# One core's decoder layer, three edits: moving operands at one offset in SBUF, state space transfers begun by Pool, exponent differences on the vector engine

## The chip, the core and the metric

The kernel runs on one core of a Trainium2 chip. The metric is the device time of one execution in microseconds (us); the profile shown here is of one execution of the kernel before the change. Lower is better.

## What is computed

The program is a chain of two transformer-like blocks on 512 tokens of width 1024, all in 32-bit floats:

```python
h = x + 0.5 * swiglu(rmsnorm(x), g1, u1, d1)                 # ffn1, hidden width 2816
# attention: compressed, selected and windowed branches (o_a), sliding window with sinks (o_b)
merged = sigmoid(ga) * (o_a @ w_branch_a) + sigmoid(gb) * (o_b @ w_branch_b)
h = h + merged @ w_out
h = h + 0.5 * swiglu(rmsnorm(h), g2, u2, d2)                 # ffn2
h = rmsnorm(h)
# second block: a gated linear recurrence of 4 heads (hgrn2) beside a state space layer (s5)
mixed = concat([hgrn2(q, f, i, g), s5(u)]) @ w_out_2
h = h + gt1 * mixed
# peer: per token and head the best 16 of 128 x 128 experts
act = gelu(einsum(h2, u_tab[idx]));  h = h + gt2 * einsum(gates * act, v_tab[idx])
out = rmsnorm(h)
```

## The kernel before

**Products.** Activations lie transposed, 8 tiles of 128 x 512 (features in partitions, tokens along them). A product with full precision is made of three passes of a faster type: an operand is split into a high part (`hi`, a cast on ACT) and a low part (`lo`, a subtraction on DVE), and `mm3` multiplies high by high, low by high and high by low. The weight tile is the stationary operand (loaded, PEld), the activation the moving one, 512 columns at a time. `weight` (L165) loads one 128 x 1024 weight tile over the SP queue, casts it on ACT (L171) and subtracts on DVE (L172). `Weights` keeps two tiles ready ahead; tiles `raw`, `whi`, `wlo` have three buffers each.

**Order.** Each stage has a main generator that issues the products and side generators that are woven in: `yield 6000` in a side generator means "go on when 6000 ns of matmul time, by the kernel's own count, have been issued". The framework under it then orders each engine's queue by its own estimates of when instructions are ready. Each engine works its queue in order, so an instruction that waits holds what stands behind it.

**Stages** (names used below, with their time in the trace): ffn1 (to 394 us), att (394 to 840), ffn2 (840 to 1247), mix (1247 to 1553), peer1 (1553 to 2440) and peer2 (to the end). Each opens a pool of SBUF tiles with `open` and closes it; the pools of all stages begin above the same resident tiles. The moving operands are:

- `xhi`, `xlo`: the normalised input of a stage, resident, used by the first products of every stage. The program lays them at byte 75,648 of each partition and on, every one 1,920 bytes past a multiple of 2,048.
- `ahi`, `alo` (ffn1, ffn2), `t` (att, mix), `pwh`, `pwl` (peer2): made inside a stage, in its pool. By the addresses that the program gives them they lie 736 (ffn1), 544 (att), 1,280 (ffn2), 928 (mix) and 704 (peer2) bytes past a multiple of 2,048.

All are 2,048 bytes a partition. Weight tiles `whi` and `wlo` lie 1,920 past a multiple of 2,048 too, and the eight 128-column slices of each follow at steps of 512 bytes.

**The end of att.** Eight branch products go into `merged`, one tile each: DVE (L812) scales, Pool (L814) adds, ACT and DVE split (L588, L589). The eight output products `wout` each need all eight `merged` tiles and begin with the first.

**The state space preparation** (`s5_prepare`) runs beside ffn2. It makes matrices for four quarters of the state space and writes them to DRAM; `s5_load` reads them back in mix. A quarter issues 24 transfers: 2 of transposed matrices (`first`), 2 of `ca`, 2 x 8 that place a triangle `ks` into a zeroed tile `T`, 2 of `T`, 1 of `cs` and 1 of `d`. All stand on ACT's queue (`nc.scalar.dma_start`; L1156 is the line of the 16). The arithmetic is Pool's (`g`) and DVE's (`v`); PE multiplies `ca` by `bz`, a spread copy of `bb`.

**The recurrence** (`hg_head`, in mix) makes for each of 4 heads and each of 7 levels two differences of a running sum (helper line L996), their exponent on ACT (L1281), and two multiplications on DVE (L1282, L1283), before PE multiplies. `s5_quarter` (four, one after another) alternates PE, DVE and Pool.

Of the kernel before, what the change touches and what calls it, by code (L numbers as in the profile page):

```python
# [8 lines left out]
F32 = mybir.dt.float32  # L9
F32R = mybir.dt.float32r  # L10
# [8 lines left out]
T = 512  # L19
D = 1024  # L20
DT = 8
# [28 lines left out]
class Prog:  # L50
# [92 lines left out]
        self.n += 1  # L143
        return f"{s}{self.n}"

    def open(self, name):
        self.phase_cm = self.tc.tile_pool(name=name, bufs=1, reuse_waits="tile")
        self.ph = self.phase_cm.__enter__()

    def close(self):  # L150
        self.phase_cm.__exit__(None, None, None)
# [542 lines left out]
    def attention(self, st, done):  # L694
        nc, A, ph = self.nc, self.A, self.ph
# [48 lines left out]

        sg, merged = [[], []], []

        def main():
            win = A["win_t"]
            order = [win[i] for i in range(8)] + [(A["win_n"][c], 688) for c in range(4)]
# [4 lines left out]
            W = Weights(self, order)  # L754
# [50 lines left out]
            for b, key, o in ((1, "ob", ob), (0, "oa", oa)):  # L805
                yield has(key)
                for m in range(DT):
                    ps = self.ps()
                    w = next(W)
                    yield from self.product(ps, w, o)  # L810
                    x = sg[b][m]
                    nc.vector.scalar_tensor_tensor(x, x, 1.0, ps, op0=ALU.add, op1=ALU.mult)  # L812
                    if b == 0:
                        nc.gpsimd.tensor_tensor(x, x, sg[1][m], op=ALU.add)  # L814
                        hl = self.t2k(F32R), self.t2k(F32R)
                        self.split(x, *hl)
                        merged.append(hl)
            for m in range(DT):
                ps = self.ps()
                w = next(W)  # L820
                yield from self.product(ps, w, merged)
                done(m, ps)
# [193 lines left out]
    def s5_prepare(self):  # L1016
# [81 lines left out]
        yield 8000  # L1098
        for i in range(2):
            s = slice(64 * i, 64 * i + 64)  # L1100
            v.tensor_copy(bz[s, :, :, 16 * i:16 * i + 16], bb[s])
        di = ph.tile([32, 16, 16], F32, name="di")
        v.tensor_tensor(di, m["eye16"][:, None, :].to_broadcast([32, 16, 16]),
                        m["s5d"][:, :, None].to_broadcast([32, 16, 16]), op=ALU.mult)
        for j in range(4):
            q = slice(4 * j, 4 * j + 4)
            first, second = self.s5d[j]
            sh = [128, 4, 8, 16]
            f4 = lambda t: t.rearrange("p (g l h) -> p g l h", g=4, l=8)
            pr, pi = (pd[:, i, :, q].rearrange("p l g -> p g l")[:, :, :, None].to_broadcast(sh) for i in range(2))  # L1110
            br, bi = (bb[:, i, q, :][:, :, None, :].to_broadcast(sh) for i in range(2))
            t, R = self.t2k(), [self.t2k(), self.t2k()]
            self.mul(g, f4(R[0]), pr, br)
            self.mul(g, f4(t), pi, bi)
            self.sub(g, R[0], R[0], t)
            self.mul(g, f4(R[1]), pr, bi)
            self.mul(g, f4(t), pi, br)
            self.add(g, R[1], R[1], t)
            yield 20000
            for i in range(2):  # L1120
                ps = self.ps()
                for a in range(4):
                    s = slice(a * 128, (a + 1) * 128)
                    self.tr(ps[:, s], R[i][:, s], self.ident)
                o = self.t2k()
                self.evac(o, ps)
                nc.scalar.dma_start(first[:, 512 * i:512 * i + 512], o)
            sh = [128, 4, 9, 16]
            pr, pi = (pw[:, i, :, q].rearrange("p l g -> p g l")[:, :, :, None].to_broadcast(sh) for i in range(2))
            pnb = pn[:, :, q].rearrange("p l g -> p g l")[:, :, :, None].to_broadcast(sh)  # L1130
            cr, ci = (m["s5c"][:, i, q, :][:, :, None, :].to_broadcast(sh) for i in range(2))
            ca = [ph.tile(sh, F32, tag="ca", bufs=3, name=self.name("ca")) for _ in range(3)]
            flat = lambda t: t.rearrange("p g l h -> p (g l h)")
            self.mul(g, ca[0], pr, cr)
            self.mul(g, ca[2], pi, ci)
            self.sub(g, flat(ca[0]), flat(ca[0]), flat(ca[2]))
            self.mul(g, ca[1], pnb, cr)
            self.mul(g, ca[2], pr, ci)
            self.sub(g, flat(ca[1]), flat(ca[1]), flat(ca[2]))
            yield 22000  # L1140
            for i in range(2):
                nc.scalar.dma_start(second[:, 1024 + 576 * i:1600 + 576 * i], flat(ca[i]))
            ps = self.ps()
            for a in range(4):
                o = ps[0:32, a * 128:(a + 1) * 128]
                for i in range(2):
                    self.mm(o, lhsT=bz[:, i, 4 * j + a, :], rhs=ca[i][:, a, 0:8, :], start=(i == 0), stop=(i == 1))
            ks = self.t2k()[0:32].rearrange("p (g x) -> p g x", g=4)
            v.tensor_copy(ks, ps[0:32].rearrange("p (g x) -> p g x", g=4))
            v.tensor_tensor(ks[:, :, 0:16], ks[:, :, 0:16], di[:, q, :], op=ALU.add)  # L1150
            for i in range(2):
                T = self.t2k()
                g.memset(T, 0.0)
                tv = T.rearrange("p (g x) -> p g x", g=4)
                for l in range(8):
                    nc.scalar.dma_start(tv[16 * l:16 * l + 16, :, 16 * l:128], ks[16 * i:16 * i + 16, :, 0:128 - 16 * l])  # L1156
                nc.scalar.dma_start(second[:, 512 * i:512 * i + 512], T)
            yield 6000

            a, k = self.t2k(), self.t2k()  # L1160
            f3 = lambda t: t.rearrange("p (g c) -> p g c", c=64)
            ang = a[:, 0:256]
            v.tensor_tensor(f3(ang), m["r8"][:, q, None].to_broadcast([128, 4, 64]),
                            m["iota"][:, None, :].to_broadcast([128, 4, 64]), op=ALU.mult)
            cs = self.t2k()
            for i, turn in enumerate((0.25, 0.0)):
                yield 4000
                self.reduce_angle(a[:, 256:512], ang, k[:, 0:256], turn)
                nc.scalar.activation(cs[:, i * 256:(i + 1) * 256], a[:, 256:512], AF.Sin)
            nc.scalar.dma_start(first[:, 1024:1536], cs)  # L1170
            d = self.t2k()
            dv = d.rearrange("p (i g c) -> p i g c", i=2, g=4)
            v.tensor_copy(dv, m["rho"][:, None, q, None].to_broadcast([128, 2, 4, 64]))
            v.memset(dv[:, :, :, 0:1], 0.0)
            nc.scalar.dma_start(first[:, 1536:2048], d)
            yield 6000


# [9 lines left out]
    def s5_quarter(self, j, un, r, ys):  # L1188
# [8 lines left out]
                                 rhs=self.ident[:, lp:128:2], start=True, stop=True)  # L1197
        U = self.t2k()
        self.evac(U, ps)
        yield 1000  # L1200
        ps = self.ps()
        for i in range(2):
            for gq in range(8):
# [1 line left out]
                self.mm(ps[64 * g2:64 * g2 + 64, i * 256 + a * 64:i * 256 + a * 64 + 64],  # L1205
                                 lhsT=r["RT"][i][:, a * 128 + 64 * g2:a * 128 + 64 * g2 + 64],
                                 rhs=U[:, gq * 64:gq * 64 + 64], start=True, stop=True)
        yield 0
        cos = r["cs"][:, None, 0:256].to_broadcast([128, 2, 256])
        sin = r["cs"][:, None, 256:512].to_broadcast([128, 2, 256])  # L1210
        h2 = lambda t: t.rearrange("p (i x) -> p i x", i=2)
        a, b, z, x = self.t2k(), self.t2k(), self.t2k(), self.t2k()
        v.tensor_tensor(h2(a), h2(ps), cos, op=ALU.mult)
        v.tensor_tensor(h2(b), h2(ps), sin, op=ALU.mult)
        self.add(g, z[:, 0:256], a[:, 0:256], b[:, 256:512])
        self.sub(g, z[:, 256:512], a[:, 256:512], b[:, 0:256])
        v.tensor_tensor_scan(x, r["d"], z, 0.0, op0=ALU.mult, op1=ALU.add)
        a, b, z = self.t2k(), self.t2k(), self.t2k()
        v.tensor_tensor(h2(a), h2(x), cos, op=ALU.mult)
        self.mul(g, h2(b), h2(x), sin)  # L1220
        zv, av, bv = i4(z), i4(a), i4(b)
        g.memset(zv[:, :, :, 0:1], 0.0)
        self.sub(g, zv[:, 0, :, 1:64], av[:, 0, :, 0:63], bv[:, 1, :, 0:63])
        self.add(g, zv[:, 1, :, 1:64], av[:, 1, :, 0:63], bv[:, 0, :, 0:63])
        yield 8000
        yn = ph.tile([64, 8, 8, 16], F32, tag="yn", bufs=1, name=self.name("yn"))
        for g2 in range(2):
            ps = self.ps()
# [36 lines left out]
    def hg_head(self, hd, q, k, b, vn, os, have_v):  # L1265
# [6 lines left out]
        def level(l):  # L1272
# [3 lines left out]
            mid = bv[:, :, 0, H - 1:H].to_broadcast([128, 256 // H, H])  # L1276
            e = self.t2k()
            ev = blk(e)
            self.sub(g, ev[:, :, 0, :], mid, bv[:, :, 0, :])
            self.sub(g, ev[:, :, 1, :], bv[:, :, 1, :], mid)  # L1280
            nc.scalar.activation(e, e, AF.Exp)  # L1281
            v.tensor_tensor(ev[:, :, 0, :], blk(k)[:, :, 0, :], ev[:, :, 0, :], op=ALU.mult)  # L1282
            v.tensor_tensor(ev[:, :, 1, :], blk(q)[:, :, 1, :], ev[:, :, 1, :], op=ALU.mult)  # L1283
# [9 lines left out]
        for l in range(7):  # L1293
# [7 lines left out]
            if l == 3:  # L1301
# [4 lines left out]
                v.tensor_copy(dec, qe[:, 127:512:128])  # L1306
                v.tensor_tensor(qe, qe, q, op=ALU.mult)
                last = c4(b)[:, :, 127:128].to_broadcast([128, 4, 128])
                self.sub(g, c4(kd), last, c4(b))
                nc.scalar.activation(kd, kd, AF.Exp)  # L1310
                v.tensor_tensor(kd, kd, k, op=ALU.mult)
            yield 2200
# [289 lines left out]
    def peer(self, st, done):  # L1602
# [2 lines left out]
        self.gd = self.dram.tile([T // GB, 128, 128, GB], F32, name="gates_d")  # L1605
        NE = 128
        gs = [self.dram.tile([128, 512], F32, name=f"act_d{e}") for e in range(NE)]
        self.open("peer1")
        self.n_t2k = 6
        xs = []  # L1610
        box = {}
# [29 lines left out]
        self.spawn(work())  # L1641
        self.weave(early())
        self.close()
        self.open("peer2")
        self.n_t2k = 4
        f = lambda x: x.rearrange("p (b t) -> p b t", t=GB)
        gts, acts = {}, {}
# [59 lines left out]
def program(tc, A, out, dbg=None, stop=None):  # L1707
    with ExitStack() as ctx:
# [3 lines left out]
        h = [P.const.tile([128, 512], F32, name=f"h{d}") for d in range(DT)]  # L1712
        rope_cm = tc.tile_pool(name="rope", bufs=1, reuse_waits="tile")
        P.rp = rope_cm.__enter__()
        P.open("ffn1")
        st = P.norm_start()
        W = P.ffn_weights(A["g1"], A["u1"], A["d1"])
        for d in range(DT):
# [12 lines left out]
            P.dump(f"h1_{d}", h[d])  # L1731
        if stop == "ffn1":
            return
        P.open("att")
        P.n_t2k = 44
        P.active = 2
        P.att_order = [3, 2, 4, 5, 6, 7, 1, 0]
# [12 lines left out]
            P.dump(f"h2_{d}", h[d])  # L1750
        if stop == "att":
            return
        P.open("ffn2")
        P.n_t2k = 9
        P.mid_start(vec["norm_final"], vec["norm_mix_w_2"])
        W = P.ffn_weights(A["g2"], A["u2"], A["d2"])
# [5 lines left out]
        P.weave(P.ffn(h, st3, W,  # L1762
                      lambda m, half: P.mid_tile(m, half, h, vec["norm_final"], vec["norm_mix_w_2"], st4), halves=True))
        P.close()
        P.open("mix")
        P.n_t2k = 31
        P.mix_consts()
        st5 = {"hi": [], "lo": [], "ready": []}
# [142 lines left out]
```

## Time and profile before

| | us |
|---|---|
| median of 3 runs | 3177.6 (3174.46 to 3178.54) |
| the profiled execution, its own time | 3182.49 |
| span from its first to its last instruction | 3180.5 |

| engine | busy us | share of the span |
|---|---|---|
| PE (matmul) | 3061.3 | 96% |
| DVE | 2044.6 | 64% |
| ACT | 1164.7 | 37% |
| POOL | 1084.8 | 34% |

The granted TensorE clock has a mean of 0.98 of full speed over the span. Matmuls overlap in the profile (a 512-column one lasts some 390 ns and the next starts after some 230), so their pace is read from start to start.

### The profile page before, as it was taken

Reading aid. Unit: us, or ns where it says so; the run is one execution under the profiler, and the core shown is the slowest. Engines: PE = TensorE matmul, PEld = TensorE weight load, DVE = VectorE, ACT = ScalarE, POOL = GpSimd, SP = SyncE. Lnnn points to the kernel's source line nnn. Section 1 sums busy time; section 2 is a strip of 40 time slices with the busy share of each in tenths; the row PEclk is TensorE's granted clock in tenths of the full one; section 3 lists DMA queues with packets and bytes.
Section 4 is the critical chain, followed back from the end, with each engine's and each line's share of the span. In section 5 each row is a group of like instructions: output and inputs, shape, how many; then the busy total and the mean of one; then the engine's idle time right before and its main releaser. Section 6 shows DMA issues by size and latency. Waiting matters only on the chain.

```text
span 3180.5 us, 39943 instructions
## 1 busy us (share of the span) xinstructions
PE 3061.3 (96%) x14672; PEld 2493.6 (78%) x14672; DVE 2044.6 (64%) x3733; ACT 1164.7 (37%) x1851; POOL 1084.8 (34%) x993
## 2 busy tenths in 40 slices
PE   8999998889999999999999988999999999999998
PEld 7888875567777778878888777888887788888887
DVE  7445466754657565864665899888883666555653
ACT  4222334442422224543433343445453333322332
POOL 1000110001222222431254689878771533223321
PEclk9999999999999999989999999999999999999999
DMA  6344331112435444221333344555556765555642
GB/s 197 118 131 136 94 96 47 34 47 86 160 101 170 131 141 133 85 77 54 100 121 116 103 150 168 189 188 188 191 186 225 244 200 184 185 194 193 201 135 78
DMA packets 145059, 443.53 MB, mean 139 GB/s; under 512 B 20177, under 2 KB 22257, under 8 KB 139745
## 3 DMA queue, kind: packets, MB, share of 16 engines
q1 hardware_dynamic: 82512, 285.41, 28.0%
q10 hardware_dynamic: 51968, 111.57, 9.7%
q0 software_dynamic: 10384, 44.01, 4.5%
q8 instruction: 116, 1.90, 0.2%
q14 instruction: 79, 0.64, 0.1%
HBM read 361.88 MB, written 77.86 MB: 138 GB/s over the span
## 4 chain that ended last, share of the span: by engine, by line
PE 78%; DVE 11%; issue 4%; ACT 2%; POOL 2%; DMA 2%; ACTq 0%; SPq 0%; DVEq 0%; POOLq 0%
PE ps L82 77%; DVE wlo L172 2%; DVE b L1543 1%; PE ps L86 1%; DMA aw<-ada_w 1%; ACT whi L171 1%; DVE stage L1568 1%; DMA act_d<-t 1%; DVE sel L1526 0%; DVE mx L896 0%; POOL t L814 0%; DVE aa L521 0%; ACTq L1156 0%; POOL a L1542 0%; DVE eq L1519 0%
## 5 line engine op out<-in xcount | busy, mean ns | idle before, releaser
L171 ACT CAST whi<-raw 128x1024 fp32r<-128x1024 f32 (+2 forms) x505 | 516.6, 1025 | 1210.2 <-PE ps L82 918.3
L82 PE MATMUL ps<-xhi,whi 128*128 128x512 f32 (+1 forms) x2232 | 879.0, 395 | 26.0 <-ACT whi L171 14.5
L82 PE MATMUL ps<-xhi,wlo 128*128 128x512 f32 (+1 forms) x2232 | 868.1, 390 | 8.2 <-DVE wlo L172 8.2
L82 PE MATMUL ps<-xlo,whi 128*128 128x512 f32 (+1 forms) x2232 | 869.4, 390 | 0.8 <-DVE xlo L380 0.7
L172 DVE TENSOR_TENSOR wlo<-raw,whi 128x1024 fp32r<-128x1024 f32 (+2 forms) x470 | 596.7, 1270 | 161.2 <-ACT whi L171 151.4
L82 PEld LDWEIGHTS ps<-xhi,whi 128*128 128x128 f32 x2232 | 425.4, 191 | 117.2 <-ACT whi L171 15.4
L82 PEld LDWEIGHTS ps<-xhi,wlo 128*128 128x128 f32 x2232 | 424.3, 190 | 99.3 <-DVE wlo L172 10.5
L82 PEld LDWEIGHTS ps<-xlo,whi 128*128 128x128 f32 x2232 | 425.2, 191 | 81.4 <-issue 2.1
L1542 POOL TENSOR_SCALAR a<-iota,routeT 128x128 fp32r<-128x128 f32 x512 | 439.6, 874 | 103.1 <-PE ps L82 97.2
L82 PE MATMUL ps<-pwl,whi 128*128 128x512 f32 (+1 forms) x1048 | 408.6, 390 | 2.8 <-DVE pwl L589 2.8
L82 PE MATMUL ps<-pwh,whi 128*128 128x512 f32 (+1 forms) x1048 | 406.8, 388 | 3.3 <-ACT pwh L588 3.2
L82 PE MATMUL ps<-pwh,wlo 128*128 128x512 f32 (+1 forms) x1048 | 403.1, 385 | 0.0
L1660 POOL TENSOR_TENSOR t<-t,gt 128x512 f32<-128x512 f32 x128 | 201.5, 1593 | 419.2 <-DMA t<-act_d 317.7
L1543 DVE SCALAR_TENSOR_TENSOR b<-iota,routeT,routeG 128x256 fp32r<-128x256 f32 x512 | 251.8, 541 | 46.0 <-PE ps L82 46.0
L82 PEld LDWEIGHTS ps<-pwh,whi 128*128 128x128 f32 x1048 | 197.4, 188 | 48.1 <-ACT pwh L588 4.6
L1794 DVE SCALAR_TENSOR_TENSOR h<-ps,mod,h 128x512 f32<-128x512 f32 (+1 forms) x131 | 96.3, 735 | 214.8 <-PE ps L82 214.8
L82 PEld LDWEIGHTS ps<-pwl,whi 128*128 128x128 f32 x1048 | 197.6, 189 | 42.3 <-DVE pwl L589 4.5
L82 PEld LDWEIGHTS ps<-pwh,wlo 128*128 128x128 f32 x1048 | 197.4, 188 | 42.5 <-DVE wlo L172 0.4
L1567 ACT COPY stage<-ps 128x256 f32<-128x256 f32 x256 | 138.1, 643 | 174.3 <-PE ps L82 138.1
L589 DVE TENSOR_TENSOR pwl<-t,pwh 128x512 fp32r<-128x512 f32 x128 | 144.8, 1160 | 40.0 <-ACT pwh L588 35.9
L266 POOL TENSOR_TENSOR acc<-acc,sq 128x512 f32<-128x512 f32 x18 | 32.3, 1796 | 391.2 <-ACT sq L262 390.8
L1568 DVE TENSOR_TENSOR stage<-stage,ps 128x256 f32<-128x256 f32 x256 | 147.3, 623 | 8.2 <-ACT stage L1567 8.1
(401 smaller groups left out, 3859.6 us busy)
## 6 DMA issues: line engine op xcount, KB each, us to landing
raw<-pu SPq DMA_DIRECT2D x128, 512.0 KB, 3.5
raw<-pv SPq DMA_DIRECT2D x128, 512.0 KB, 3.5
act_d<-t ACTq DMA_DIRECT2D x128, 256.0 KB, 2.4
gates_d<-stage ACTq DMA_DIRECT2D x32, 1024.0 KB, 4.6
gt<-gates_d POOLq DMA_DIRECT2D x16, 2048.0 KB, 14.6
t<-act_d ACTq DMA_DIRECT2D x128, 256.0 KB, 3.6
aw<-ada_w SPq DMA_DIRECT2D x48, 512.0 KB, 4.5
raw<-g SPq DMA_DIRECT2D x44, 512.0 KB, 3.6
```

The source lines that it names most:

```text
L82: self.nc.tensor.matmul(out, lhsT=lhsT, rhs=rhs, start=start, stop=stop)
L86: self.nc.tensor.transpose(out, x, ident)
L171: nc.scalar.copy(hi[:, :n], raw[:, :n])
L172: (nc.gpsimd if self.pool_lo else nc.vector).tensor_tensor(lo[:, :n], raw[:, :n], hi[:, :n].bitcast(F32), op=ALU.subtract)
L266: nc.gpsimd.tensor_tensor(st["acc"], st["acc"], sq, op=ALU.add)
L589: self.nc.vector.tensor_tensor(lo, x, hi.bitcast(F32), op=ALU.subtract)
L1542: g.tensor_scalar(a[:, i, :], iota, T2[0][:, c], None, op0=ALU.is_equal)
L1543: v.scalar_tensor_tensor(b[:, i], iota[:, None, :].to_broadcast([128, 2, 128]), T2[1][:, c], TG[:, t + i, :, None].to_broadcast([128, 2, 1 ...
L1567: nc.scalar.copy(sv, pv[:, :, 0])
L1568: v.tensor_tensor(sv, sv, pv[:, :, 1], op=ALU.add)
L1660: g.tensor_tensor(f(t), f(t), gts[e // 8][:, :, e % 8, :], op=ALU.mult)
L1794: nc.vector.scalar_tensor_tensor(x, ps, P.mod[:, 40 + d:41 + d], x, op0=ALU.mult, op1=ALU.add)
```

## The change

1. `open` takes a number of bytes and lays an unused tile `pad` of that size first in each stage's pool, so that all later tiles of the pool move up: ffn1 by 1,184, att by 1,376, ffn2 by 640, mix by 992, peer1 by 128, peer2 by 1,216 bytes. In ffn1, att, ffn2, mix and peer2 the moving operands of the stage then lie 1,920 bytes past a multiple of 2,048.
2. At the end of att the split of a `merged` tile becomes a side generator that goes on 3400 ns later, and the first two `wout` products are made together: first tiles 0 to 5 of both, then tiles 6 and 7 of both.
3. The 24 transfers of a quarter in `s5_prepare` go from ACT's queue to Pool's, two copies into `bz` from DVE to Pool, and waits in matmul time change (20000 to 13000, 22000 to 15000, a new 5000 ahead of each sine).
4. `s5_quarter` gets other and more places at which it yields.
5. In `hg_head` the two differences of each level and one of 128 x 512 per head go from Pool to DVE.

```diff
-    def open(self, name):
+    def open(self, name, pad):
         self.phase_cm = self.tc.tile_pool(name=name, bufs=1, reuse_waits="tile")
         self.ph = self.phase_cm.__enter__()
+        self.ph.tile([128, pad // 4], F32, name="pad")
...
+        def halves(x):
+            yield 3400
+            hl = self.t2k(F32R), self.t2k(F32R)
+            self.split(x, *hl)
+            merged.append(hl)
...
                         nc.gpsimd.tensor_tensor(x, x, sg[1][m], op=ALU.add)
-                        hl = self.t2k(F32R), self.t2k(F32R)
-                        self.split(x, *hl)
-                        merged.append(hl)
-            for m in range(DT):
+                        self.spawn(halves(x))
+
+            ws, pss = [W.take(hold=True) for _ in range(2)], [self.ps(), self.ps()]
+            for ks in (range(6), range(6, 8)):
+                for m in range(2):
+                    _, hi, lo = ws[m]
+                    for k in ks:
+                        if len(merged) <= k:
+                            yield lambda: len(merged) > k
+                        s = slice(k * 128, (k + 1) * 128)
+                        self.mm3(pss[m], hi[:, s], lo[:, s], merged[k][0], merged[k][1], k == 0, k == 7)
+                        if k % 2:
+                            yield
+                    if k == 7:
+                        W.prep()
+                        done(m, pss[m])
+            for m in range(2, DT):
...
-            v.tensor_copy(bz[s, :, :, 16 * i:16 * i + 16], bb[s])
+            g.tensor_copy(bz[s, :, :, 16 * i:16 * i + 16], bb[s])
...
-            yield 20000
+            yield 13000
...
-                nc.scalar.dma_start(first[:, 512 * i:512 * i + 512], o)
+                g.dma_start(first[:, 512 * i:512 * i + 512], o)
...
-            yield 22000
+            yield 15000
...
-                    nc.scalar.dma_start(tv[16 * l:16 * l + 16, :, 16 * l:128], ks[16 * i:16 * i + 16, :, 0:128 - 16 * l])
-                nc.scalar.dma_start(second[:, 512 * i:512 * i + 512], T)
+                    g.dma_start(tv[16 * l:16 * l + 16, :, 16 * l:128], ks[16 * i:16 * i + 16, :, 0:128 - 16 * l])
+                g.dma_start(second[:, 512 * i:512 * i + 512], T)
...
                 self.reduce_angle(a[:, 256:512], ang, k[:, 0:256], turn)
+                yield 5000
                 nc.scalar.activation(cs[:, i * 256:(i + 1) * 256], a[:, 256:512], AF.Sin)
...
-        yield 1000
+        yield 2400
...
-        yield 0
+        yield 700
...
+        yield 1700
         self.add(g, z[:, 0:256], a[:, 0:256], b[:, 256:512])
         self.sub(g, z[:, 256:512], a[:, 256:512], b[:, 0:256])
+        yield 1800
         v.tensor_tensor_scan(x, r["d"], z, 0.0, op0=ALU.mult, op1=ALU.add)
...
+        yield 1600
         self.mul(g, h2(b), h2(x), sin)
...
-        yield 8000
+        yield 4500
...
-            self.sub(g, ev[:, :, 0, :], mid, bv[:, :, 0, :])
-            self.sub(g, ev[:, :, 1, :], bv[:, :, 1, :], mid)
+            self.sub(v, ev[:, :, 0, :], mid, bv[:, :, 0, :])
+            self.sub(v, ev[:, :, 1, :], bv[:, :, 1, :], mid)
...
-                self.sub(g, c4(kd), last, c4(b))
+                self.sub(v, c4(kd), last, c4(b))
...
-        self.open("peer1")
+        self.open("peer1", 128)
...
-        self.open("peer2")
+        self.open("peer2", 1216)
...
-        P.open("ffn1")
+        P.open("ffn1", 1184)
...
-        P.open("att")
+        P.open("att", 1376)
...
-        P.open("ffn2")
+        P.open("ffn2", 640)
...
-        P.open("mix")
+        P.open("mix", 992)
```

## Rows read from the trace of the kernel before

**Rows 1.** The page's chain of work that ended last, by engine.
```profile
PE 78%; DVE 11%; issue 4%; ACT 2%; POOL 2%; DMA 2%; ACTq 0%; SPq 0%; DVEq 0%; POOLq 0%
```

**Rows 2.** Busy time by stage: length, engines' busy us (count), granted clock, DMA.
```profile
394.00:840.00 446.00, 410.08 (x1979) 295.52 (x1979) 265.57 (x603) 181.05 (x457) 42.49 (x28) 0.95 0.21 65
840.00:1247.00 407.00, 392.13 (x1826) 322.62 (x1825) 251.43 (x373) 119.72 (x159) 96.86 (x80) 0.98 0.45 140
1247.00:1553.00 306.00, 290.14 (x1858) 244.30 (x1857) 194.41 (x346) 138.62 (x212) 91.13 (x112) 0.95 0.26 86
2480.00:3180.00 700.00, 691.91 (x3103) 570.65 (x3101) 404.84 (x400) 206.25 (x256) 216.67 (x138) 1.00 0.55 179
```

**Rows 3.** Timeline of PE: starts of resident operands' matmuls (start us, us).
```profile
330.17 0.39 PE L82 MATMUL ps<-xhi,whi 128*128 128x512 f32 x1
...
335.61 0.39 PE L82 MATMUL ps<-xhi,whi 128*128 128x512 f32 x1
```

**Rows 4.** Timeline of PE: starts of the stages' own operands' matmuls (ffn1, att, peer2).
```profile
206.43 0.40 PE L82 MATMUL ps<-ahi,wlo 128*128 128x512 f32 x1
...
211.34 0.40 PE L82 MATMUL ps<-ahi,wlo 128*128 128x512 f32 x1
...
805.15 0.64 PE L82 MATMUL ps<-t,whi 128*128 128x512 f32 x2
...
811.48 0.63 PE L82 MATMUL ps<-t,whi 128*128 128x512 f32 x2
...
2600.40 0.39 PE L82 MATMUL ps<-pwh,whi 128*128 128x512 f32 x1
...
2605.90 0.39 PE L82 MATMUL ps<-pwh,whi 128*128 128x512 f32 x1
```

**Rows 5.** Waits of PE from 762 to 840 us (total us, times, longest).
```profile
PE ps L82 <- ACT t L588: 4.7, 2, 2.7
```

**Rows 6.** Busy time and granted clock behind four waits, columns as in rows 2.
```profile
795.00:802.00 7.00, 4.33 (x10) 2.78 (x10) 3.89 (x5) 2.69 (x4) 2.17 (x1) 0.52 0.25 80
886.00:898.00 12.00, 7.42 (x22) 5.60 (x21) 9.93 (x9) 3.64 (x5) 10.23 (x8) 0.72 0.19 65
...
1128.00:1140.00 12.00, 6.78 (x19) 4.61 (x18) 10.75 (x15) 4.92 (x7) 7.07 (x5) 0.72 0.42 136
...
1403.00:1423.00 20.00, 20.00 (x101) 14.06 (x102) 8.58 (x15) 6.27 (x11) 3.46 (x5) 0.50 0.17 57
```

**Rows 7.** Waits of PE, then of DVE, in ffn2.
```profile
PE ps L82 <- DVE wlo L172: 8.9, 4, 4.6
PE ps L82 <- ACT whi L171: 5.5, 3, 4.9
...
DVE bbz L1101 <- POOL bb L999: 7.5, 1, 7.5
```

**Rows 8.** The 64 triangle transfers on ACT's queue, and who waited for them.
```profile
L1156 ACTq DMA_DIRECT2D t<-t x64: 567/607/1572, 962.3 to 1207.8; - x64
...
  ACT ahi L588: 29.9, 2
```

**Rows 9.** Groups on POOL: issuing transfers (busy us, mean ns | idle before).
```profile
L1652 POOL DMA_DIRECT2D gt<-gates_d x16 | 27.6, 1726 | 52.2 <-DMA act_d<-t 45.8 <-DMA t<-act_d 2.9 <-POOL t L1660 2.4
...
L1183 POOL DMA_DIRECT2D s5y<-s5m x4 | 2.3, 564 | 16.1 <-PE ps L82 16.1
```

**Rows 10.** Waits of PE in mix.
```profile
PE ps L82 <- DVE t L1283: 5.5, 3, 3.8
```

**Rows 11.** Groups of the recurrence: differences on POOL, multiplications on DVE.
```profile
L996 POOL TENSOR_TENSOR t<-t 128x256 f32<-128x256 f32 x56 | 38.7, 720 | 36.1 <-DVE t L1256 36.1
...
L1282 DVE TENSOR_TENSOR t<-t,t 128x256 f32<-128x256 f32 x28 | 18.1, 648 | 10.3 <-ACT t L1281 10.3
```

**Rows 12.** Timeline in mix: L1282 with Pool at work, and without.
```profile
1289.95 0.86 DVE L1282 TENSOR_TENSOR t<-t,t 128x256 f32<-128x256 f32 x1
...
1305.42 0.41 DVE L1282 TENSOR_TENSOR t<-t,t 128x256 f32<-128x256 f32 x1
```

More of the change, by code (lines that the diff above doesn't have):

```diff
@@ L1139, in s5_prepare @@
             self.sub(g, flat(ca[1]), flat(ca[1]), flat(ca[2]))
-            yield 22000
+            yield 15000
             for i in range(2):
-                nc.scalar.dma_start(second[:, 1024 + 576 * i:1600 + 576 * i], flat(ca[i]))
+                g.dma_start(second[:, 1024 + 576 * i:1600 + 576 * i], flat(ca[i]))
             ps = self.ps()
@@ L1168, in s5_prepare @@
                 self.reduce_angle(a[:, 256:512], ang, k[:, 0:256], turn)
+                yield 5000
                 nc.scalar.activation(cs[:, i * 256:(i + 1) * 256], a[:, 256:512], AF.Sin)
-            nc.scalar.dma_start(first[:, 1024:1536], cs)
+            g.dma_start(first[:, 1024:1536], cs)
             d = self.t2k()
@@ L1174, in s5_prepare @@
             v.memset(dv[:, :, :, 0:1], 0.0)
-            nc.scalar.dma_start(first[:, 1536:2048], d)
+            g.dma_start(first[:, 1536:2048], d)
             yield 6000
```

## The prediction

> **What bounds the kernel now.** I read the page first. TensorE is the engine of 78% of the chain that ended last, and the other engines' shares are a few waits, not a second bound [rows 1]. So a saving must come from three places: a shorter spacing between matmuls, less waiting of PE, or less time at a low granted clock. I then read the stages as windows: att, ffn2 and mix leave PE idle for 36, 15 and 16 us and have mean clocks of 0.95, 0.98 and 0.95, while peer2 leaves 8 us at 1.00 [rows 2]. Next I took PE's timeline where it waits for nothing, since matmuls overlap and only starts show their pace; then the waits of PE in the three stages; then the clock right behind the longest of them; last the groups of ACT, Pool and DVE that the change touches.
>
> **Edit 1, the pads.** A resident operand's 24 matmuls take 5.44 us from first to last start: 226.7 ns each [rows 3]. A stage's own operands are slower: 21 in 4.91 us in ffn1 (233.8 ns), 27 in 6.33 us in att (234.4), 24 in 5.50 us in peer2 (229.2) [rows 4]. All are 512 columns wide at full clock. The one difference that I find in the program is the offset. If the pads give every operand 226.7 ns, 528 products of ffn1 (22 tiles x 8 x 3), 384 of att, 456 of ffn2 and 168 of mix, counted from the loops, gain 7.1 to 7.7 ns each (ffn2 and mix priced by ffn1 and att), 11.2 us; peer2's 3,000 gain 2.5 ns each, 7.5 us. That is 18.7 us. Where PE waits for something else the gain is lost, so I take 17.5. The lower end is 0, because offset 704 (peer2) costs 2.5 ns and offset 736 (ffn1), 32 bytes from it, costs 7.1: offset alone does not order them. For peer1's one-hot operands and the half-width products no row shows a pace against an offset; 932 matmuls by the largest difference seen, 7.7 ns, bound them at 7 us either way. I take 0.
>
> The Trainium skill, "SBUF — State Buffer", section "Who interferes with whom", says that PE and ACT never wait on anyone there. By that sentence an operand's place would not matter, and the 17.5 would be 0. The rows above show a pace that differs by operand, which the sentence does not explain; they do not show that place is the reason.
>
> **Edit 2, the end of att.** PE waits 4.7 us there for ACT's split of the merged tiles [rows 5]. The split waits for Pool's addition to the same tile, 2.17 us for one, and from 795 to 802 us the granted clock is 0.52 while PE is busy for 4.33 us [rows 6]; at full clock that work takes 2.25 us, so 2.1 more are lost. Together 6.8. After the change 2 x 6 x 3 = 36 matmuls (8.2 us at 226.7 ns) need only the first six tiles. What is late next is the last merged tile: Pool's 2.17 us, then a cast and a subtraction; if each took as long as the addition, 6.5 in all, below 8.2. The new 3400 ns gap is matmul time, and it takes the split out from ahead of later branch work in ACT's and DVE's queues. I take 6.5; the ends are 0 (the split itself becomes late) and 7.
>
> **Edit 3, Pool issues the transfers.** In ffn2 PE waits 8.9 us for `wlo` and 5.5 for `whi` [rows 7]. The longest of these have one kind of cause. ACT's queue holds 64 triangle transfers of 0.607 us, 39 us of issuing, in a row and behind landings; an `ahi` cast there waited 29.9 us in two waits [rows 8], and weight casts stand behind it. And DVE's copy into `bz` stood 7.5 us waiting for Pool [rows 7] with a weight subtraction behind it. Behind two of these the clock is 0.72 for 12 us each [rows 6]: with levels of 1.2 and 2.4 GHz, half and full speed, that is 6.7 us at half, worth 3.4 us, twice. So 14.4 + 6.8 = 21.2 us can be had. Nothing on PE's weight path remains behind a transfer.
>
> What it costs: Pool gets 96 issues. No row shows these on Pool. The nearest are 0.564 us (4 of `s5y`, the same kind of small copy between tile and DRAM) and 1.726 us (`gt`, the dearest that Pool issues) [rows 9]. I take 0.56: 54 us onto Pool's 97 busy of 407 [rows 2]; at 1.73 it is 166 and Pool still fits. But behind an issue that waits for a landing now stand `ca`, the next quarter's arithmetic and the fills of `T`, and PE's products of `ca` wait for these. `ca` is due 15000 ns of matmul time after its start, not 22000. I allow 1 us of PE's waiting in each quarter, 4 in all; if the cover is gone (Pool late by a whole 0.56 x 16 = 9 us in each quarter) it is 36. The two `bz` copies are 2 us on an idle Pool, hidden. I take 21.2 - 4, rounded up to 18 for the smaller waits of the same kind; ends -15 and 22.
>
> The same page of the Trainium skill, section "SBUF: two separate sides", warns against transfers from Pool's queue: while VectorE holds the shared port pair, descriptors can't be written, and it gives about 620 ns alone and 3100 overlapped. An estimate by that page: 96 x 2.5 us = 240 us more on Pool. The 0.564 us of `s5y`, taken in mix with DVE at work, does not show it; four issues are few.
>
> **Edits 4 and 5, mix.** The stage lasts 306 us and PE is busy for 290.1 at a mean clock of 0.95 [rows 2]. PE's largest wait is 3.8 us for `t` of L1283 [rows 10], near 1397 us: the recurrence's differences stand on Pool behind an addition of `s5_quarter` that waits for DVE, the exponents behind these, the multiplications behind those. From 1403 to 1423 the clock is 0.50 [rows 6], which loses 10 us. So 14 us hang on this one place, and all idle time with all clock loss (306 x 0.05) is 31.
>
> The price: 56 differences leave Pool, where they took 38.7 us (720 ns), with 36.1 us of waits [rows 11]. On DVE the nearest form is L1282, same shape: 0.86 us with Pool at work, 0.41 without [rows 12]. So DVE gains 56 x 0.41 = 23 to 56 x 0.65 = 36 us, and some 3 for the four 128x512 ones. In return the multiplications, 648 ns in the mean [rows 11], fall towards 410 when Pool is not beside them: 56 x 0.24 = 13 us back. Net 13 to 27 us on DVE's 194.4 of 306 [rows 2], which is room in the mean. The new wait: a multiplication behind the exponent on ACT, after two differences on the same queue. Queued behind it on DVE are weight subtractions; PE has them ready two tiles ahead. The longer yields of `s5_quarter` come to some 4 us a quarter, 15 in all, and finish before the last products need the result as long as the quarters don't end the stage. I take 10 of the 14; the ends are -10 and +27.
>
> **Sum.** 17.5 + 6.5 + 18 + 10 = 52 us. The profiled execution took 3182.5 (span 3180.5 and 2.0 around it), so it would come to 3130.5. The median of the runs shown is 4.9 below the profiled one, so 52 less than 3177.6 is 3125.6: 3126.
>
> **Rivals.**
>
> *A. The pads do nothing*: the slow pace belongs to the tiles (their writers, the mix of work beside them), not to the place. For: 704 and 736 bytes price so differently; against: the operands of ffn1 and att are slow by nearly the same, in the company of very different work. 52 - 17.5 = 34.5: 3143.
>
> *D. DVE becomes the bound in mix*: each level's chain of two differences, exponent and two multiplications is now DVE, ACT, DVE, and DVE's weight subtractions stand behind. It decides where PE's lead of two weight tiles (48 matmuls, 11 us at 226.7 ns) is less than what DVE has queued. Then DVE's 27 us come onto the path in place of the 10: 52 - 37 = 15: 3163. For: DVE is the busiest engine beside PE; against: 64% busy.
>
> *C. Pool's issue is dear, slower than before.* Pool has 407 - 97 = 310 us free in ffn2. With the 29.9 us that ACT waited behind landings [rows 8] it becomes the end of ffn2 from (310 - 30) / 96 = 2.9 us an issue. At 3.5 us: 97 + 30 + 336 = 463, 56 more than the stage, and the 18 are not won: 3126 + 18 + 56 = 3200. For: no row shows the triangle form on Pool, with starts in the middle of the partitions; against: both rows of issues on Pool lie below 1.8 us.
>
> *E. Another order on the queues*: a place in ffn2 or mix gets a new wait with 10 us of half clock behind it, as the old one had. It takes the size of one place, 14 us: 3140, inside the forecast's range.
>
> **Chances.** The forecast with E 0.62 (own range 3108 to 3146), A 0.17, D 0.14 (with A also, 3180, no change), C 0.07. Low end: all bounds in favour, 18.7 + 7 + 22 + 27 = 75, gives 3103; rounded to 3100 for the half-width products. High end: D's 3163 with 3 for a Pool a little late, 3166. A difference under 0.2%, 6.4 us, is about what a measurement here cannot tell from no change. Slower needs C's turning point (0.07, less a small part that only eats the gain): 0.06. Same: D with A, and C near its turning point: 0.05. Faster: 0.89.
>
> **What the profile after would show.** Pads: starts of `ahi`, `t`, `pwh` 226 to 227 ns apart; if still 234, A. Att: no wait of PE for L588 near 790 to 800 us and no stretch at 0.52. Ffn2: no L1156 on ACT's queue, that line on Pool near 0.56 us; PE's waits for `wlo` and `whi` below 5 us together, the 0.72 stretches gone; a wait of PE for `ca` or `ks` of over 4 us a quarter makes edit 3 wrong, as does an issue of over 2.9 us. Mix: L1282 near 410 ns, DVE's busy time at 207 to 221 us, no stretch of 20 us at 0.50; a wait of PE for DVE that is longer than 5.5 us in sum makes edit 5 wrong. The step I trust least is that offset alone sets the pace; the next is that mix gets no new wait in the place of the old.

## The result

The changed kernel takes 3136.44 us (median of 4 runs, 3134.93 to 3138.35), the kernel before 3178.07 beside it (4 runs): ratio 0.9867, interval 0.9849 to 0.9885, or 41.6 us less. The forecast was 3126 in a range of 3100 to 3166. The profiled execution took 3137.6; its span is 3135.8.

The chain of work that ended last, by engine (of the changed kernel, as in [rows 1]):

```profile
PE 84%; DVE 10%; ACT 2%; issue 2%; DMA 1%; POOL 1%; SPq 0%; ACTq 0%; DVEq 0%; POOLq 0%
```

PE's share of the chain grew from 78% to 84%. Where the time went is seen by stages. For the table I took PE's timeline and measured from landmark to landmark: first `ahi` matmul, last `ahi` matmul of ffn1, last `t` by `wlo` matmul of att, last `ahi` of ffn2, last `t` by `wlo` of mix, first `pwh` matmul, last one. Each row is the one profiled execution of a kernel (us), the last column the median of all its runs; all but `before` and `after` are experiments of the next section.

| kernel | ffn1 | att | ffn2 | mix | peer1 | peer2 | median of all runs |
|---|---|---|---|---|---|---|---|
| before | 302.6 | 454.0 | 408.9 | 297.2 | 910.3 | 713.5 | 3178 |
| pads_only | 299.2 | 446.4 | 405.8 | 288.2 | 910.7 | 707.1 | 3165.7 |
| att_only | 302.6 | 448.1 | 407.8 | 293.5 | 909.3 | 713.3 | 3173.7 |
| prep_only | 302.6 | 453.4 | 389.9 | 295.9 | 910.6 | 715.0 | 3161.8 |
| mix_only | 302.6 | 453.1 | 408.8 | 287.2 | 910.7 | 713.3 | 3171.2 |
| after | 299.2 | 448.4 | 387.2 | 286.8 | 911.5 | 707.1 | 3136.4 |
| no_pads | 302.6 | 452.7 | 390.4 | 287.0 | 910.1 | 713.0 | 3147.3 |
| heads01_pool | 299.2 | 447.2 | 387.1 | 280.0 | 911.6 | 707.5 | 3128.8 |

From before to after: ffn1 -3.4, att -5.6, ffn2 -21.7, mix -10.4, peer1 +1.2, peer2 -6.4. By the forecast's terms the savings were 3.7, 9.5, 21.2, 11.3, 0 and 7.5. The six differences come to 46.3 us, more than the 41.6 of the medians: the profiled execution of the kernel before was 4.4 us above its median, that of the changed kernel 1.1.

In the changed kernel line numbers are larger by 2 from L149 on, by more behind the later edits: L588 is L590, L1156 is L1178, L1282 and L1283 are L1308 and L1309, L996 is L1018, L1300 is L1326. Its windows of the same stages (columns as in [rows 2]; the last one is a stretch early in mix):

```profile
391.00:832.00 441.00, 409.36 (x1981) 297.26 (x1980) 266.20 (x606) 181.59 (x457) 42.14 (x27) 0.95 0.21 66
832.00:1217.00 385.00, 381.40 (x1823) 318.02 (x1822) 256.70 (x368) 119.67 (x158) 153.37 (x179) 1.00 0.47 148
1217.00:1503.00 286.00, 272.94 (x1787) 232.26 (x1786) 196.49 (x388) 136.69 (x202) 45.31 (x49) 0.97 0.26 88
2440.00:3130.00 690.00, 687.25 (x3109) 572.19 (x3107) 402.13 (x394) 206.06 (x257) 215.00 (x138) 1.00 0.56 180
1284.00:1302.00 18.00, 13.17 (x54) 11.10 (x54) 16.60 (x38) 4.44 (x13) 0.00 (x0) 0.62 0.18 62
```

Ffn2 has PE idle for 3.6 us in place of 14.9, at a clock of 1.00. Pool's busy time there went from 96.9 to 153.4 us: 52 us of the 96 issues (the forecast added 54) and 2.3 of the two copies. Mix keeps a weak place, from 1284 to 1302 us. So does the end of att. These are the same 15 us there before and after:

```profile
790.00:805.00 15.00, 10.08 (x33) 6.90 (x32) 7.87 (x10) 5.18 (x7) 4.35 (x2) 0.77 0.35 121
```

```profile
790.00:805.00 15.00, 13.33 (x51) 10.30 (x50) 8.25 (x10) 6.77 (x9) 4.35 (x3) 0.89 0.43 141
```

A mean clock of 0.77 is 6.9 us at half clock, 0.89 is 3.3: about half of that loss is left.

The pace (starts of the stages' own operands, answering to [rows 4]):

```profile
206.16 0.39 PE L82 MATMUL ps<-ahi,whi 128*128 128x512 f32 x1
...
211.60 0.39 PE L82 MATMUL ps<-ahi,whi 128*128 128x512 f32 x1
...
809.91 0.62 PE L82 MATMUL ps<-t,whi 128*128 128x512 f32 x2
...
815.35 0.62 PE L82 MATMUL ps<-t,whi 128*128 128x512 f32 x2
...
2599.74 0.39 PE L82 MATMUL ps<-pwh,whi 128*128 128x512 f32 x1
...
2605.18 0.39 PE L82 MATMUL ps<-pwh,whi 128*128 128x512 f32 x1
```

All three are 24 matmuls in 5.44 us, 226.7 ns each, the figure of the resident operands [rows 3]. The waits of PE at the end of att, in ffn2 and in mix (columns as in [rows 5]):

```profile
PE ps L82 <- ACT t L590: 1.4, 1, 1.4
PE ps L82 <- DVE wlo L174: 0.8, 1, 0.8
...
PE ps L82 <- DVE wlo L174: 3.0, 2, 2.0
PE ps L82 <- DVE alo L591: 0.6, 1, 0.6
...
PE ps L82 <- DVE t L1326: 5.3, 3, 2.6
PE ps L82 <- DVE t L1309: 3.2, 2, 2.0
```

The groups of the moved work, on Pool in ffn2 and on DVE in mix, as in [rows 9, 11]:

```profile
L1178 POOL DMA_DIRECT2D t<-t x64 | 34.3, 543 | 17.1 <-DVE t L568 17.1
...
L1018 DVE TENSOR_TENSOR t<-t 128x256 f32<-128x256 f32 x56 | 20.8, 416 | 0.0
L1308 DVE TENSOR_TENSOR t<-t,t 128x256 f32<-128x256 f32 x28 | 12.7, 453 | 0.6 <-ACT t L1307 0.4
L1309 DVE TENSOR_TENSOR t<-t,t 128x256 f32<-128x256 f32 x28 | 12.2, 435 | 0.0
...
L1018 DVE TENSOR_TENSOR t<-t 128x512 f32<-128x512 f32 x4 | 2.7, 682 | 0.0
```

An issue takes 0.543 us on Pool (forecast 0.56), a difference 0.416 on DVE (0.41), and the multiplications of both lines fell from 36.0 us in 56 (18.1 and, for L1283, 17.9; 644 ns) to 24.9 (444 ns).

### The profile page after: what moved, and what is told of

It reads as the page before. It is cut to its first block, busy times and chain, and to the rows that moved or that the text cites. A ratio compares the mean times of both kernels' runs of the same rounds, so it can differ in the third digit from the quotient of the medians.

```text
span 3135.8 us, 39961 instructions
## 1 busy us (share of the span) xinstructions
PE 3035.7 (97%) x14672; PEld 2489.8 (79%) x14672; DVE 2059.1 (66%) x3791; ACT 1168.3 (37%) x1853; POOL 1100.6 (35%) x1031
## 4 chain that ended last, share of the span: by engine, by line
PE 84%; DVE 10%; ACT 2%; issue 2%; DMA 1%; POOL 1%; SPq 0%; ACTq 0%; DVEq 0%; POOLq 0%
PE ps L82 83%; DVE wlo L174 2%; DVE b L1569 2%; PE ps L86 1%; DVE stage L1594 1%; DVE sel L1552 1%; ACT whi L173 1%; DVE mx L918 0%; DMA act_d<-t 0%; POOL t L823 0%; DVE eq L1545 0%; POOL a L1568 0%; ACT t L923 0%; ACT t L590 0%; DVE ps L914 0%
## 5 line engine op out<-in xcount | busy, mean ns | idle before, releaser
L82 PEld LDWEIGHTS ps<-xhi,whi 128*128 128x128 f32 x2232 | 424.3, 190 | 110.4 <-DVE stage L1594 10.4
L1568 POOL TENSOR_SCALAR a<-iota,routeT 128x128 fp32r<-128x128 f32 x512 | 446.0, 887 | 98.1 <-PE ps L82 92.3
L591 DVE TENSOR_TENSOR pwl<-t,pwh 128x512 fp32r<-128x512 f32 x128 | 152.8, 1223 | 43.5 <-ACT pwh L590 39.6
```

The costliest lines, as they stand in the source:

```text
L82: self.nc.tensor.matmul(out, lhsT=lhsT, rhs=rhs, start=start, stop=stop)
L591: self.nc.vector.tensor_tensor(lo, x, hi.bitcast(F32), op=ALU.subtract)
L1568: g.tensor_scalar(a[:, i, :], iota, T2[0][:, c], None, op0=ALU.is_equal)
```

## The experiments

**The pads, alone and left out.**

```diff
 # pads_only: before, with
+        self.ph.tile([128, pad // 4], F32, name="pad")
 # no_pads: after, without that line
```

> The kernel before with the pads alone. Theory (the place of a stage's operand sets its pace): all 512-column products of ahi, t, pwh and pwl start 226 to 227 ns apart; some 18 us less than before, of which 3.5 in ffn1, 6 to 7.5 in peer2, 1 to 3 in each of the others; the waits of PE for ACT and DVE in att, ffn2 and mix stay. Rival (the pads work only together with the other edits, or the order of the queues changes with them): a saving under 10 us, or one that does not lie in ffn1 and peer2.

> The changed kernel without its pads. If the parts add up, it is 18 us slower than the changed kernel, 3155 us, with the paces of before (234 and 229 ns) and without the waits that edits 2 to 5 removed. Rival (a shorter matmul only gives PE more to wait for in the stages that wait): 8 to 12 us slower, since only ffn1 and peer2 pay.

pads_only: 3165.66 us against 3177.64, ratio 0.9962 (0.9948 to 0.9976), 12.0 us less. no_pads: 3147.34, 10.9 us above the changed kernel. So the pads are worth 11 to 12 us, the figure of the rival for no_pads (8 to 12) and not 18. In the two pairs of the table ffn1 gains 3.4 and 3.4, ffn2 3.1 and 3.2, peer2 6.4 and 5.9, so ffn2 pays too. Att shows 7.6 and 4.3, but more than its pad differs there: its granted clock from 394 to 840 us is 0.97 in pads_only and 0.95 in the kernel before. Mix gains nothing from its pad when edits 4 and 5 are there (286.8 and 287.0). The 9 us that mix lost in the profile of pads_only are chance: of its five runs the profiled one took 3155.1, the others 3163.8 to 3166.1. In it the longest wait, 3.8 us, is still there, but the 20 us behind it have a clock of 0.91, not 0.50 [rows 6]. The wait (L1285 is L1283 of the kernel before), then the window behind it:

```profile
1387.38 1.96 PE L82 MATMUL ps<-t 128*128 128x128 f32 x8 [3.81 <-DVE t L1285]
```

```profile
1387.00:1407.00 20.00, 19.52 (x170) 14.94 (x171) 12.78 (x22) 8.69 (x14) 5.35 (x7) 0.91 0.23 83
```

**What the offset is measured against.** Two kernels move the weights or the operands.

```diff
 # wswap: after, with
-        self.w = ep(tc.tile_pool(name="w", bufs=3))
         self.big = ep(tc.tile_pool(name="big", bufs=1))
+        self.w = ep(tc.tile_pool(name="w", bufs=3))
-        self.open("peer2", 1216)
+        self.open("peer2", 0)
 # offs: after, with pads of
-    1184 (ffn1), 1376 (att),  640 (ffn2),  992 (mix), 1216 (peer2)
+    1696 (ffn1),  864 (att), 1664 (ffn2), 1120 (mix), 1280 (peer2)
```

> The changed kernel with the weight tiles laid behind the resident tiles, so that weights lie 704 past a multiple of 2048 and xhi, xlo, ahi, t still 1920; peer2 has no pad, so that pwh and pwl lie at 704, as the weights. If the pace goes by the moving operand's own place: 226.7 ns for xhi and ahi, 226 to 232 for pwh and pwl, as before. If it goes by the distance of operand and weights: 226.7 for pwh and pwl, 229 to 234 for xhi and ahi, and some 20 us slower than the changed kernel.

> The changed kernel with other pads, so that the operand lies behind the weight tile's place, taken modulo 2048, by 512 bytes in ffn1, 1536 in att, 1024 in ffn2, 128 in mix and 64 in peer2 (0 in the changed kernel). If only the same place modulo 2048 is fast: 229 to 237 ns in all five stages, some 18 us slower than the changed kernel. If the eight slices of a weight tile, 512 bytes apart, are what counts: 226.7 ns in ffn1, att and ffn2, 228 to 234 in mix and peer2, 6 to 9 us slower.

wswap took 3166.3 us (one run), 30 more than the changed kernel where some 20 were expected. PE's timeline of it, `xhi` in ffn1 and `pwh` in peer2:

```profile
329.94 0.39 PE L82 MATMUL ps<-xhi,whi 128*128 128x512 f32 x1
...
335.54 0.39 PE L82 MATMUL ps<-xhi,whi 128*128 128x512 f32 x1
...
2609.95 0.39 PE L82 MATMUL ps<-pwh,whi 128*128 128x512 f32 x1
...
2615.39 0.39 PE L82 MATMUL ps<-pwh,whi 128*128 128x512 f32 x1
```

`xhi` has not moved modulo 2,048 and is now slow: 24 in 5.60 us, 233.3 ns. `pwh` lies at 704, where it was slow before, and is fast: 24 in 5.44 us, 226.7 ns, because the weights lie at 704 too. So the pace goes by the distance between operand and weight tile. offs took 3146.8 us (one run), 10 more than the changed kernel where 6 to 9 were expected, and its timeline says which distances are fast (in this order: ffn1 at 512, att at 1,536, ffn2 at 1,024, mix at 128, peer2 at 64):

```profile
206.27 0.39 PE L82 MATMUL ps<-ahi,whi 128*128 128x512 f32 x1
...
211.71 0.39 PE L82 MATMUL ps<-ahi,whi 128*128 128x512 f32 x1
...
810.23 0.62 PE L82 MATMUL ps<-t,whi 128*128 128x512 f32 x2
...
815.67 0.62 PE L82 MATMUL ps<-t,whi 128*128 128x512 f32 x2
...
1173.64 0.39 PE L82 MATMUL ps<-ahi,whi 128*128 128x512 f32 x1
...
1179.08 0.39 PE L82 MATMUL ps<-ahi,whi 128*128 128x512 f32 x1
...
1475.10 0.62 PE L82 MATMUL ps<-t,whi 128*128 128x512 f32 x2
...
1479.75 0.62 PE L82 MATMUL ps<-t,whi 128*128 128x512 f32 x2
...
2609.98 0.39 PE L82 MATMUL ps<-pwh,whi 128*128 128x512 f32 x1
...
2615.48 0.39 PE L82 MATMUL ps<-pwh,whi 128*128 128x512 f32 x1
```

Distances of 512, 1,024 and 1,536 keep 226.7 ns (24 in 5.44 us); 128 gives 232.5 (20 in 4.65), 64 gives 229.2 (24 in 5.50). Multiples of 512, the step of the weight tile's slices, are the fast ones among the distances tried; none was a multiple of 256 alone, so whether that would do is not shown.

**Edit 2 alone.**

> The kernel before with edit 2 alone (split of the merged tiles as a side generator, two output products made together). The forecast's sum says 6.5 us less. By the changed kernel's profile, where one wait for the split is left with 3.4 us of half clock, 3 to 5 us less: 3173 to 3175 us. Rival (the stage's gain in the changed kernel is its pad's): no change within 2 us.

3173.66 us against 3178.33, ratio 0.9987 (0.9973 to 1.0001): 4.7 us, and an interval that just touches no change. Eight of its ten runs lie below all 19 of the kernel before. From 790 to 805 us the clock of its profiled execution is 1.00, where the kernel before has 0.77; one wait of 1.3 us for the split is left. In the changed kernel the same edit leaves a clock of 0.89 there. The time of the whole stage decides little here: att_only and no_pads run the same att, and it takes 448.1 and 452.7 us.

**Edit 3, alone and with its transfers back on ACT.**

```diff
 # prep_only: before, with edit 3; act_dma: after, with (and so for all 24)
-                    g.dma_start(tv[...], ks[...])
+                    nc.scalar.dma_start(tv[...], ks[...])
```

> The kernel before with the state space transfers on Pool and the waits in matmul time changed, nothing else. Theory (ACT's and DVE's queues held up the weights): ffn2 loses 17 to 20 us, the rest stays, 3158 to 3161 us. Rival (ffn2's gain in the changed kernel came from the pads and the new order): under 10 us.

> The changed kernel with the 24 transfers of a quarter back on ACT's queue; the new waits in matmul time and Pool's two copies stay. Theory (the transfers on ACT's queue held the weight casts): 10 to 15 us slower than the changed kernel, 3146 to 3151 us, with half clock in ffn2 again. Rival (the waits in matmul time and the copies made the gain): within 3 us.

prep_only: 3161.78 against 3177.64, 15.9 us less (0.9946, 0.9929 to 0.9962), with 19.0 us off ffn2. act_dma: 3145.38, 8.9 us above the changed kernel; ffn2 takes 394.9 us, 7.7 more. Its waits of PE in ffn2:

```profile
PE ps L82 <- DVE wlo L174: 6.7, 5, 2.1
PE ps L82 <- ACT whi L173: 1.4, 2, 1.2
```

The expectation of 10 to 15 was too high: with the transfers back on ACT, PE waits 8.1 us, not the 14.4 of [rows 7], and one short stretch of half clock comes back (a mean of 0.91 from 1081 to 1100 us). So 8 to 9 us are the transfers' (7.7 by ffn2, 8.9 by the medians). The rest of ffn2's 19 us belongs to the new waits in matmul time and the two copies on Pool, which no run separates. The trace of the kernel before ties most of it to the copies. DVE's timeline, then PE's:

```profile
887.35 2.66 DVE L1101 COPY bbz<-bb 64x512 f32<-64x512 f32 x2 [7.47 <-POOL bb L999]
```

```profile
892.10 0.79 PE L82 MATMUL ps<-xhi,wlo 128*128 128x512 f32 x1 [4.58 <-DVE wlo L172]
```

DVE stands 7.5 us and then copies until 890.0; the weight subtraction runs behind that, from 890.65 to 892.05, and PE waits 4.6 us for it. With the half clock of the 12 us there [rows 6], worth 3.4 us, this place cost 8.0 us. In act_dma, where the copies are Pool's, no wait of PE in ffn2 is longer than 2.1 us.

**Edits 4 and 5, together and one by one.**

```diff
 # mix_only: before, with edits 4 and 5; hg_only: with edit 5 only; s5q_only: with edit 4 only
```

> The kernel before with edits 4 and 5 alone (s5_quarter's yields, the differences on the vector engine). Theory: mix loses 8 to 10 us, 3168 to 3170 us. Rival (part of mix's gain came from the pads or from ffn2 handing over earlier): 0 to 5 us.

> The kernel before with edit 5 alone: the differences on the vector engine, the state space quarters as before. Theory (Pool's queue was the cause of the longest wait in mix and of the 20 us of half clock behind it): mix about 290 us, 6 to 10 us less in all, the whole of what edits 4 and 5 gave together (6.4). Rival (the yields of s5_quarter did it): under 2 us.

> The kernel before with edit 4 alone: the yields of s5_quarter. The differences alone gave nothing, both edits together 6.4 us. If the yields are the cause (Pool's addition no longer stands waiting ahead of the differences): 5 to 8 us less, mix near 288 us with no 20 us at half clock. If the two are needed together: under 2 us.

mix_only: 3171.20 against 3177.64, 6.4 us less (0.998, 0.997 to 0.9989), between the 8 to 10 of the theory and the rival's 0 to 5. hg_only: 3178.16 against 3178.33 (0.9994, 0.9978 to 1.0009), nothing. s5q_only: 3183.37 against 3177.87 (1.0008, 0.9994 to 1.0021), no gain either; its median is 5.5 us higher, which the interval does not tell from no change. For the single edits the figure of the theory failed each time, and neither edit alone is the cause: the gain needs the two together. The windows show it: first the one long stretch at a low clock that mix_only has in mix, early, then the longest of hg_only and of s5q_only, later and lower (three kernels, each in its own fence):

```profile
1312.00:1330.00 18.00, 12.67 (x54) 11.21 (x54) 16.60 (x38) 4.82 (x13) 0.00 (x0) 0.62 0.18 59
```

```profile
1407.00:1425.00 18.00, 18.00 (x68) 12.09 (x67) 8.37 (x19) 4.52 (x9) 0.58 (x1) 0.53 0.19 60
```

```profile
1382.00:1410.00 28.00, 22.99 (x90) 16.40 (x91) 16.36 (x22) 6.16 (x12) 9.02 (x15) 0.51 0.21 67
```

With the differences on DVE but the old yields, PE still waits up to 3.7 us, now for a copy of the state space quarter on DVE that stands behind a weight subtraction, and 18 us at 0.53 follow a later wait (this profiled execution took 3185.95 us, one of the two slowest of its ten, so a typical one may lose less). With the new yields but the differences on Pool, nine of them stand in a row on Pool, and PE waits 9.9 us in five waits for L1286 (L1283 of the kernel before). The longest, in DVE's timeline of s5q_only:

```profile
1382.25 0.94 DVE L1285 TENSOR_TENSOR t<-t,t 128x256 f32<-128x256 f32 x1
1383.11 6.45 DVE L1286 TENSOR_TENSOR t<-t,t 128x256 f32<-128x256 f32 x1
```

and Pool's beside it:

```profile
1383.46 5.82 POOL L996 TENSOR_TENSOR t<-t 128x256 f32<-128x256 f32 x9
```

**The weak place that is left.** In the changed kernel Pool is idle early in mix while DVE is busy for 16.6 of 18 us. The recurrence begins near 1250 us there, PE's longest waits for it lie between 1280 and 1297 us, and Pool's first work behind them is this:

```profile
1308.30 0.74 POOL L1021 TENSOR_TENSOR t<-t,t 128x256 f32<-128x256 f32 x1 [84.76 <-PE ps L82]
```

Two kernels give the first heads' differences back to Pool.

```diff
 # after, with (heads01_pool; head0_pool has hd == 0)
+            d = g if hd < 2 else v
-            self.sub(v, ev[:, :, 0, :], mid, bv[:, :, 0, :])
-            self.sub(v, ev[:, :, 1, :], bv[:, :, 1, :], mid)
+            self.sub(d, ev[:, :, 0, :], mid, bv[:, :, 0, :])
+            self.sub(d, ev[:, :, 1, :], bv[:, :, 1, :], mid)
```

> The changed kernel with the first head's 14 differences back on Pool, which has nothing else to do then. Theory (the four waits of PE in the first 20 us of the recurrence and the 13.6 us of half clock behind them come from VectorE's queue, which has the differences and the last rows of the second block's norm): 3 to 8 us faster than the changed kernel. Rival (they come from the chain difference, exponent, multiplication itself, which Pool makes longer): 0 to 5 us slower.

> The changed kernel with the differences of heads 0 and 1 on Pool, of 2 and 3 on the vector engine. One head on Pool gave 3.5 us and left two waits of 2.8 and 2.3 us behind vector engine work of head 1. If the vector engine's queue is the cause of these too: 2 to 5 us more, 3128 to 3131 us. If head 1's own chain is the limit, Pool's longer differences cost: 3132 to 3138 us.

head0_pool: 3132.89 us (4 runs, 3130.89 to 3135.9), ratio to before 0.9857 (0.9841 to 0.9873). Its runs overlap those of the changed kernel, and 11 us at a clock of 0.53 stay in its mix, from 1286 us on: the 3.5 us are not clear of chance. heads01_pool: 3128.76 (4 runs, 3125.82 to 3132.38), ratio to before 0.9838 (0.9809 to 0.9867), 7.7 us below the changed kernel, whose fastest run took 3134.93. Two windows of heads01_pool: the one in which PE still waits, and the one with the last levels of the first two heads, where the changed kernel has its weak place:

```profile
1258.00:1278.00 20.00, 16.36 (x91) 15.14 (x91) 20.00 (x35) 8.19 (x14) 11.22 (x15) 1.00 0.09 27
1277.00:1295.00 18.00, 18.00 (x130) 16.03 (x128) 16.90 (x37) 6.00 (x14) 0.00 (x0) 1.00 0.20 64
```

The clock stays at 1.00 where the changed kernel has 0.62, and mix takes 280.0 us instead of 286.8. This version has the lowest median of all.

## Why the prediction was right, and where its sizes were off

The sign, the range and the order of the terms held. Measured one by one, the edits give 12.0 + 4.7 + 15.9 + 6.4 = 39.0 us of the 41.6; the forecast had 17.5 + 6.5 + 18 + 10 = 52. Every term came out too large. That is clear of noise for edit 1 and for edits 4 and 5; the intervals of edits 2 and 3 alone contain their terms. The low end of the range holds a gain of 27 us in mix that no step of the forecast gives: 14 were priced there.

**Edit 1: right in the pace, off in the term, wrong in the reason.** All three paces came out at 226.7, so rival A fell. The term that was mis-sized is "I take 17.5": it counted nearly all of the gain in pace as time saved, and 12.0 and 10.9 came. Ffn1, ffn2 and peer2 gained 3.4, 3.1 and 6.4 us in the first pair, close to their 3.7, 3.2 and 7.5. In mix nothing can be told from chance, and att's figures hold differences of the clock too. That the waits of these two stages swallow their gain is likely; no run shows it by itself. The 0 for half-width products was a small loss: in peer2 the median distance of their starts is 118 ns in the kernel before and 120 in the changed one. They too go by the distance in memory, 120 ns at 0 (changed kernel, first fence) and 113.3 at 64 (offs, second fence):

```profile
3106.33 0.28 PE L82 MATMUL ps<-pwh,whi 128*128 128x256 f32 x1
...
3111.01 0.28 PE L82 MATMUL ps<-pwh,whi 128*128 128x256 f32 x1
```

```profile
3116.74 0.28 PE L82 MATMUL ps<-pwh,whi 128*128 128x256 f32 x1
...
3119.80 0.28 PE L82 MATMUL ps<-pwh,whi 128*128 128x256 f32 x1
```

(39 in 4.68 us, 27 in 3.06.) The stated reason, one place for every operand, is refuted by wswap: what counts is the place against the weights. The puzzle that the forecast left open, 704 against 736, stays open: measured from the weights these are distances of 832 and 864, neither a multiple of 512, and still 229.2 and 233.8 ns. By the sentence of the Trainium skill ("SBUF — State Buffer", "Who interferes with whom") that PE never waits on anyone there, this term would have been 0; the measurement, 226.7 against 233.3 ns for `xhi` by place alone, decides against that reading.

**Edit 2: 6.5 was 4.7.** The forecast's sign, no wait for the split and no stretch at low clock, did not come: in the changed kernel a wait of 1.4 us for ACT's split and one of 0.8 for `wlo` stay, and the 15 us there have a clock of 0.89, against 0.77 before. The 0.3 us that the forecast left for all this was too little.

**Edit 3: the stage was right (21.2 for edit and pad, 21.7 in the profiled executions), and its two causes stand.** PE's waits fell from 14.4 to 3.6 us and the clock rose to 1.00. Of the two causes that the forecast names, ACT's queue is 8 to 9 us by act_dma, and the copy into `bz` 8.0 by the trace of before; no run has the copy alone. By the medians the edit alone gave 15.9, not 18. Rival C fell: 64 issues at 543 ns, with DVE busy for two thirds of the stage. The Trainium skill ("SBUF — State Buffer", "SBUF: two separate sides") warns of 3.1 us in place of 0.62 for a transfer issued from Pool's queue beside a copy on DVE. That is not seen here, beside DVE's work in ffn2: an issue took 0.543 us, and a triangle landed 2.2 us after its issue in the median, against 1.9 from ACT's queue before.

**Edits 4 and 5: 10 was 6.4.** The price came out just under its low end: 20.8 + 2.7 us of differences came, 36.0 - 24.9 of multiplications went, 12.4 net against 13 to 27. The 20 us of half clock went too. The forecast had DVE's busy time rise by 13 to 27 us; between the table's landmarks of mix it rose from 186.0 to 197.1. What the term missed is rival D on a small scale: from 1280 to 1297 us, near the end of the first two heads, where DVE also ends the second block's norm, PE waits for L1326 and L1309, and 18 us at a clock of 0.62 go with it. The forecast called edit 5 wrong if PE's waits for DVE came to more than 5.5 us; these two lines have 8.5, each alone less than 5.5. That a mean of 64% busy leaves room was true of the stage and false of this stretch. Rival E is the same event under its other name: it said 3140, nearer to the 3136.4 than the forecast's 3126. That is partly luck, since the other terms were too large as well. And the forecast's step that the differences' queue alone caused the long wait was wrong: without the new yields, moving them changes nothing.

## What to carry to other kernels

Where matmuls follow each other without a gap, compare their pace operand by operand, and look at the distance in SBUF between moving operand and weights before looking for work to remove. Price a wait of PE with the granted clock behind it, but as a range: the same wait of 3.8 us had 20 or 3 us at half clock behind it. Balance two engines by stretch and not by stage: the engine that was rightly relieved in most of mix was idle for 85 us around the first two heads, and giving it their differences back was worth 7.7 us.

## What the hardware showed that I had not expected

A 512-column matmul starts 226.7 ns after the one before when moving operand and weight tile lie a multiple of 512 bytes apart (0, 512, 1,024 and 1,536 modulo 2,048), and 229 to 234 at the other distances seen here (64, 128, 672, 832, 864, 1,216). With 256 columns, in peer2, it is the other way round, 120 ns at distance 0 and 113.3 at 64. Why is open.

A multiplication of 128x256 on DVE took 6.45 us, not 0.42, beside nine differences in a row on Pool (5.82 us), and ended 0.28 us after Pool's row had. Another in the same trace, at 1346.22 us, took 4.29 beside six (3.65) and ended 0.29 us after them. So one operation can lose a whole row, as far as two cases show. In the mean such an operation took 644 ns in the kernel with the differences on Pool and 444 in the one without.
